# Average pooling by four: loads of 63 KB and one-piece stores in place of loads of 64 KB and two-piece stores

## The chip, the core and the metric

The kernel runs on one core of a Trainium2 chip. The metric is the device time of one execution in microseconds (us); shorter is better. The time before is the median of three runs, 1557.35 us (1557.14 to 1557.62).

A core has several engines that run side by side. Here VectorE (DVE) adds, ScalarE (ACT) multiplies by a quarter, and SyncE (SP) and ScalarE issue DMAs, which 16 DMA engines carry out between DRAM and the 128 partitions of the on-chip memory. DMAs issued by SP are on queue q1 of the profile, those issued by ACT on q10.

## What is computed

```python
def reference(x, kernel_size, stride):      # x: (64, 256, 8192) float32, both numbers are 4
    out_len = (length - kernel_size) // stride + 1
    for i in range(out_len):
        start = i * stride
        output[:, :, i] = np.mean(x[:, :, start : start + kernel_size], axis=2)
```

Window and stride are both 4 and 8192 is a multiple of 4, so every four neighbours of the flattened input give one output. The input is 536.87 MB, the output 134.22 MB.

## The kernel before

The flat input is cut into 64 blocks of 8 MB. In each block every one of the 128 partitions has a run of 16,384 contiguous elements (`RUN`, 64 KB), and gives 4,096 results (16 KB).

There are two input tiles `xt` of 64 KB per partition (pool `xin`) and two result tiles `r` of 2 x 16 KB (pool `res`); a tile is taken by turns, and its new writer waits until the readers of its old contents are done. The main loop takes two blocks to one result tile:

- `load` (L43) is issued by SP. Load i waits until the reduce of block i - 2 has freed its input tile.
- `sums` (L47) is one VectorE reduce that adds each group of four into a half of `r`. The first reduce into a result tile waits for the store that last read it, two groups ago.
- `scale` (L65) multiplies the whole of `r` by 1/4 on ScalarE, in place.
- The store (L77) is issued by ScalarE. Its DRAM side (`both`) has two 16 KB pieces for each partition, 2 MB apart, one in each block.

The last four blocks are handled apart. For the last group of the loop, scale and store come after the loads of the last two blocks have been issued, and the store goes through SP (L87). Block 62 is reduced, scaled and stored by itself (L90). Block 63 is loaded in two pieces of 10,240 and 6,144 elements (`LAST`); each is summed by `pair_sums`, two VectorE additions, scaled, and stored by SP (L95). `pair_sums` first adds neighbours in place, leaving the sums on every other element (L56), and then adds those sums in pairs, reading every fourth element (L60).

Each engine executes its instructions in program order. Nothing but the waits on tiles orders one engine against another.

Of the kernel before, what the change touches and what calls it, by code (L numbers as in the profile page):

```python
# [1 line left out]

# [4 lines left out]


RUN = 16384

LAST = (10240, 6144)


@with_exitstack
def kernel(
    ctx: ExitStack,
    tc: tile.TileContext,
    x: bass.AP,
    kernel_size: bass.AP,
    stride: bass.AP,  # L20
    out: bass.AP,
):
    nc = tc.nc
    K, S = int(kernel_size), int(stride)
    assert K == S == 4
    B, C, L = x.shape
    P = nc.NUM_PARTITIONS
    dt = x.dtype
    M = RUN // K
    blocks = B * C * L // (P * RUN)  # L30
    assert blocks * P * RUN == B * C * L and L % K == 0 and blocks % 2 == 0
    assert sum(LAST) == RUN

    xb = x.rearrange("b c l -> (b c l)").rearrange("(n p m) -> n p m", p=P, m=RUN)
    ob = out.rearrange("b c l -> (b c l)").rearrange("(n p m) -> n p m", p=P, m=M)

    pin = ctx.enter_context(tc.tile_pool(name="xin", bufs=2))
    pout = ctx.enter_context(tc.tile_pool(name="res", bufs=2))

    def load(i, a=0, b=RUN, xt=None):  # L40
        if xt is None:
            xt = pin.tile([P, RUN], dt, name="xt")
        nc.sync.dma_start(out=xt[:, a:b], in_=xb[i][:, a:b])  # L43
        return xt

    def sums(o, xt, a=0, b=RUN):
        nc.vector.tensor_reduce(  # L47
            out=o,
            in_=xt[:, a:b].rearrange("p (m k) -> p m k", k=K),
            axis=mybir.AxisListType.X,  # L50
            op=mybir.AluOpType.add,
        )

    def pair_sums(o, xt, a, b):
        v = xt[:, a:b].rearrange("p (m k) -> p m k", k=2)
        nc.vector.tensor_tensor(  # L56
            out=v[:, :, 0], in0=v[:, :, 0], in1=v[:, :, 1], op=mybir.AluOpType.add
        )
        w = xt[:, a:b].rearrange("p (m k) -> p m k", k=K)
        nc.vector.tensor_tensor(  # L60
            out=o, in0=w[:, :, 0], in1=w[:, :, 2], op=mybir.AluOpType.add
        )

    def scale(o):
        nc.scalar.mul(o, o, 1.0 / K)  # L65

    def both(i):
        return ob[i : i + 2].rearrange("n p m -> p n m")

    for i in range(0, blocks - 2, 2):  # L70
        r = pout.tile([P, 2, M], dt, name="r")
        for h in range(2):
            xt = load(i + h)
            sums(r[:, h, :], xt)
        if i < blocks - 4:
            scale(r[:])
            nc.scalar.dma_start(out=both(i), in_=r[:])  # L77

    n = blocks - 1
    t = pout.tile([P, 2, M], dt, name="r")  # L80
    xt = load(n - 1)
    xl = None
    edges = [sum(LAST[:j]) for j in range(len(LAST) + 1)]
    for a, b in zip(edges[:-1], edges[1:]):
        xl = load(n, a, b, xl)
    scale(r[:])
    nc.sync.dma_start(out=both(n - 3), in_=r[:])  # L87
    sums(t[:, 0, :], xt)
    scale(t[:, 0, :])
    nc.sync.dma_start(out=ob[n - 1], in_=t[:, 0, :])  # L90
    for a, b in zip(edges[:-1], edges[1:]):
        o = t[:, 1, a // K : b // K]
        pair_sums(o, xl, a, b)
        scale(o)
        nc.sync.dma_start(out=ob[n][:, a // K : b // K], in_=o)  # L95


# [1 line left out]
_INS = ['x', 'kernel_size', 'stride']  # L99
_OUTS = [((64, 256, 2048), 'float32')]  # L100

_NUMBERS = {'kernel_size': 4, 'stride': 4}


# [26 lines left out]
```

## Time and profile before

| | |
|---|---|
| median of the runs | 1557.35 us |
| the profiled execution | 1557.44 us |
| its span, first to last instruction | 1555.7 us |
| DVE busy | 1101.1 us, 71% |
| ACT busy | 226.6 us, 15% |
| one reduce of a block, L47 | 17.22 us, 63 of them |
| one scale of a group, L65 | 7.03 us, 31 of them |
| DMA from issue to landing, a 64 KB load | 31.0 us median |
| DMA from issue to landing, a store of a group (L77) | 49.5 us median |
| DRAM traffic over the span | 431 GB/s |

The span runs from the first to the last instruction of the program; the time of the execution is a little longer. "Busy" leaves out waiting and the issuing of DMAs. In a timeline line, the first number is the start, the second the duration, both in us; `SPq` and `ACTq` are the issuing of a DMA; the square bracket has the engine's idle time before the instruction and what ended it. In a line of stretches the columns are the stretch, its length, busy time and number of instructions of DVE, ACT and POOL, the clock of TensorE (not used here), the busy share of the DMA engines, and GB/s.

A packet, in this text, is one record of the DMA part of the trace: one DMA engine moving one partition's contiguous row. Each DMA also has 16 packets of 4 bytes that report its completion, one for each engine.

### The profile page before, as it was taken

The page shows a single profiled execution, that of the slowest core. Times are in us where ns is not written, and L with a number is a line of the kernel's source. Part 1 is how long each engine was busy: PE and PEld are TensorE (multiplying, and loading weights), DVE is VectorE, ACT ScalarE, POOL GpSimd, SP SyncE. Part 2 cuts the span into 40 slices and gives each one's busy share as a digit, 9 for nine tenths or more (in the row PEclk, how much of TensorE's full clock was granted, in tenths as well). Part 3 has the DMA queues.
Part 4 walks back from the last instruction along what each step waited for, and adds up shares of the span by engine and source line. Part 5 has one row for each costly group of instructions (what it writes and reads, how often), then busy time and mean ns, then how long its engine had stood idle before and what let it go on. Part 6 is the DMA issues. An engine that isn't in the chain of part 4 may idle for free.

```text
span 1555.7 us, 398 instructions
## 1 busy us (share of the span) xinstructions
DVE 1101.1 (71%) x67; ACT 226.6 (15%) x35; POOL 0.2 (0%) x4
## 2 busy tenths in 40 slices
DVE  4858667677676776767768677676786766867668
ACT  0110111101111001111011110111101111011111
POOL 0000000000000000000000000000000000000000
DMA  9999999999999999999999999999999999999999
GB/s 425 395 429 435 437 439 431 431 423 436 437 431 438 436 428 431 437 429 441 438 435 429 433 424 443 431 433 436 434 428 436 431 436 436 434 435 431 434 428 399
DMA packets 18227, 671.12 MB, mean 431 GB/s; under 512 B 1584, under 2 KB 1584, under 8 KB 1712
## 3 DMA queue, kind: packets, MB, share of 16 engines
q1 hardware_dynamic: 10064, 545.26, 81.1%
q10 hardware_dynamic: 8160, 125.83, 18.9%
q14 instruction: 3, 0.02, 0.0%
HBM read 536.87 MB, written 134.22 MB: 431 GB/s over the span
## 4 chain that ended last, share of the span: by engine, by line
DMA 64%; DVE 35%; ACT 1%; issue 0%; SPq 0%; DVEq 0%
DMA xt<-in_x_dram 60%; DVE r L47 34%; DMA out_dram<-r 3%; DVE xt L56 1%; ACT r L65 1%; DVE r L60 0%; SPq L43 0%; DVEq L47 0%
## 5 line engine op out<-in xcount | busy, mean ns | idle before, releaser
L47 DVE TENSOR_REDUCE r<-xt 128x4096 f32<-128x16384 f32 x63 | 1084.8, 17220 | 448.5 <-DMA out_dram<-r 241.4
L65 ACT ACTIVATE r<-r 128x8192 f32<-128x8192 f32 (+3 forms) x34 | 225.3, 6628 | 1323.8 <-DVE r L47 1313.5
L56 DVE TENSOR_TENSOR xt<-xt 128x5120 f32<-128x5120 f32 (+1 forms) x2 | 8.8, 4420 | 0.0
L60 DVE TENSOR_TENSOR r<-xt 128x2560 f32<-128x2560 f32 (+1 forms) x2 | 7.6, 3776 | 0.1
L65 ACT ACT_TABLE_LOAD x1 | 1.3, 1283 | 0.7 <-PEq L112 0.7
L112 POOL MEMSET const-bfloat16-1.0<- 128x1 bf16 x1 | 0.1, 101 | 0.0
L112 POOL MEMSET const-uint8-127<- 128x1 uint8 x1 | 0.1, 101 | 0.0
L112 POOL MEMSET const-float32-0.0<- 128x1 f32 x1 | 0.1, 98 | 0.2 <-issue 0.2
L112 POOL MEMSET const-float32-1.0<- 128x1 f32 x1 | 0.1, 98 | 0.0
## 6 DMA issues: line engine op xcount, KB each, us to landing
out_dram<-r ACTq DMA_DIRECT2D x30, 4096.0 KB, 49.5
xt<-in_x_dram SPq DMA_DIRECT2D x1, 5120.0 KB, 19.6
out_dram<-r SPq DMA_DIRECT2D x1, 4096.0 KB, 29.6
xt<-in_x_dram SPq DMA_DIRECT2D x1, 3072.0 KB, 26.6
out_dram<-r SPq DMA_DIRECT2D x1, 2048.0 KB, 12.8
out_dram<-r SPq DMA_DIRECT2D x1, 1280.0 KB, 7.0
xt<-in_x_dram SPq DMA_DIRECT2D x63, 31.0
out_dram<-r SPq DMA_DIRECT2D x1, 768.0 KB, 3.5
```

The lines of the kernel that those rows point to most:

```text
L47: nc.vector.tensor_reduce(out=o, in_=xt[:, a:b].rearrange("p (m k) -> p m k", k=K), axis=mybir.AxisListType.X, op=mybir.AluOpType.add,)
L56: nc.vector.tensor_tensor(out=v[:, :, 0], in0=v[:, :, 0], in1=v[:, :, 1], op=mybir.AluOpType.add)
L60: nc.vector.tensor_tensor(out=o, in0=w[:, :, 0], in1=w[:, :, 2], op=mybir.AluOpType.add)
L65: nc.scalar.mul(o, o, 1.0 / K)
L112: nc = _bacc.Bacc("TRN2", target_bir_lowering=False, num_devices=1)
```

## The change

- The run of a load becomes 16,128 elements (63 KB). Two loads, h = 0 and 1, now read the two halves of a run of 32,256 contiguous elements (126 KB) of each partition, so that the results of a group are 8,064 contiguous elements of DRAM for each partition. The store of a group has one piece of 31.5 KB for each partition.
- There are 32 such groups (64 loads). What is left of the input is one block of 16,384 contiguous elements for each partition (`END`), loaded in the same two pieces `LAST` as before.
- The first load of all is issued as two of 8,064 elements for each partition (`FIRST`), and each half is reduced when it has landed.
- `pair_sums` writes its first sums compactly to the front of the piece, and its second addition reads neighbours there, that is every other element.
- In the last group, each half is scaled by itself. Its second half is summed by `pair_sums` in place of the reduce. All its loads and those of the last block are issued ahead of its store, which goes through SP.

The tiles stay as they were in number: `xt` has 16,384 elements for each partition, `r` has 8,064.

```diff
-RUN = 16384
+RUN = 16128
+END = 16384
+FIRST = (8064, 8064)
 LAST = (10240, 6144)
...
-    xb = x.rearrange("b c l -> (b c l)").rearrange("(n p m) -> n p m", p=P, m=RUN)
-    ob = out.rearrange("b c l -> (b c l)").rearrange("(n p m) -> n p m", p=P, m=M)
+    xb = xf[:body].rearrange("(n p h m) -> n p h m", p=P, h=2, m=RUN)
+    ob = of[: body // K].rearrange("(n p m) -> n p m", p=P, m=2 * M)
+    xe = xf[body:].rearrange("(p m) -> p m", p=P)
+    oe = of[body // K :].rearrange("(p m) -> p m", p=P)
...
     def pair_sums(o, xt, a, b):
         v = xt[:, a:b].rearrange("p (m k) -> p m k", k=2)
+        h = xt[:, a : (a + b) // 2]
         nc.vector.tensor_tensor(
-            out=v[:, :, 0], in0=v[:, :, 0], in1=v[:, :, 1], op=mybir.AluOpType.add
+            out=h, in0=v[:, :, 0], in1=v[:, :, 1], op=mybir.AluOpType.add
         )
-        w = xt[:, a:b].rearrange("p (m k) -> p m k", k=K)
+        w = h.rearrange("p (m k) -> p m k", k=2)
         nc.vector.tensor_tensor(
-            out=o, in0=w[:, :, 0], in1=w[:, :, 2], op=mybir.AluOpType.add
+            out=o, in0=w[:, :, 0], in1=w[:, :, 1], op=mybir.AluOpType.add
         )
...
-    for i in range(0, blocks - 2, 2):
-        r = pout.tile([P, 2, M], dt, name="r")
+    for g in range(groups):
+        r = pout.tile([P, 2 * M], dt, name="r")
         for h in range(2):
-            xt = load(i + h)
-            sums(r[:, h, :], xt)
-        if i < blocks - 4:
+            xt = None
+            for a, b in edges(FIRST) if g + h == 0 else [(0, RUN)]:
+                xt = load(xb[g, :, h, :], a, b, xt)
+                o = r[:, h * M + a // K : h * M + b // K]
+                if g == groups - 1 and h == 1:
+                    pair_sums(o, xt, a, b)
+                else:
+                    sums(o, xt, a, b)
+                if g == groups - 1:
+                    scale(o)
+        if g < groups - 1:
             scale(r[:])
-            nc.scalar.dma_start(out=both(i), in_=r[:])
+            nc.scalar.dma_start(out=ob[g], in_=r[:])
...
-    scale(r[:])
-    nc.sync.dma_start(out=both(n - 3), in_=r[:])
-    sums(t[:, 0, :], xt)
-    scale(t[:, 0, :])
-    nc.sync.dma_start(out=ob[n - 1], in_=t[:, 0, :])
-    for a, b in zip(edges[:-1], edges[1:]):
-        o = t[:, 1, a // K : b // K]
+    for a, b in edges(LAST):
+        xl = load(xe, a, b, xl)
+    nc.sync.dma_start(out=ob[groups - 1], in_=r[:])
+    e = pout.tile([P, 2 * M], dt, name="r")
+    for a, b in edges(LAST):
+        o = e[:, a // K : b // K]
         pair_sums(o, xl, a, b)
         scale(o)
-        nc.sync.dma_start(out=ob[n][:, a // K : b // K], in_=o)
+        nc.sync.dma_start(out=oe[:, a // K : b // K], in_=o)
```

More of the change, by code (lines that the diff above doesn't have):

```diff
@@ L29, with load, sums @@
     M = RUN // K
-    blocks = B * C * L // (P * RUN)
-    assert blocks * P * RUN == B * C * L and L % K == 0 and blocks % 2 == 0
-    assert sum(LAST) == RUN
-    xb = x.rearrange("b c l -> (b c l)").rearrange("(n p m) -> n p m", p=P, m=RUN)
-    ob = out.rearrange("b c l -> (b c l)").rearrange("(n p m) -> n p m", p=P, m=M)
+    total = B * C * L
+    groups = total // (2 * P * RUN)
+    body = groups * 2 * P * RUN
+    assert L % K == 0 and total - body == P * END
+    assert sum(FIRST) == RUN and sum(LAST) == END
+    xf = x.rearrange("b c l -> (b c l)")
+    of = out.rearrange("b c l -> (b c l)")
+    xb = xf[:body].rearrange("(n p h m) -> n p h m", p=P, h=2, m=RUN)
+    ob = of[: body // K].rearrange("(n p m) -> n p m", p=P, m=2 * M)
+    xe = xf[body:].rearrange("(p m) -> p m", p=P)
+    oe = of[body // K :].rearrange("(p m) -> p m", p=P)
     pin = ctx.enter_context(tc.tile_pool(name="xin", bufs=2))
     pout = ctx.enter_context(tc.tile_pool(name="res", bufs=2))
-    def load(i, a=0, b=RUN, xt=None):
+    def load(src, a, b, xt=None):
         if xt is None:
-            xt = pin.tile([P, RUN], dt, name="xt")
-        nc.sync.dma_start(out=xt[:, a:b], in_=xb[i][:, a:b])
+            xt = pin.tile([P, END], dt, name="xt")
+        nc.sync.dma_start(out=xt[:, a:b], in_=src[:, a:b])
         return xt
-    def sums(o, xt, a=0, b=RUN):
+    def sums(o, xt, a, b):
         nc.vector.tensor_reduce(
@@ L65, in scale, with edges @@
         nc.scalar.mul(o, o, 1.0 / K)
-    def both(i):
-        return ob[i : i + 2].rearrange("n p m -> p n m")
-    for i in range(0, blocks - 2, 2):
-        r = pout.tile([P, 2, M], dt, name="r")
-        for h in range(2):
-            xt = load(i + h)
-            sums(r[:, h, :], xt)
-        if i < blocks - 4:
+    def edges(cuts):
+        at = [sum(cuts[:j]) for j in range(len(cuts) + 1)]
+        return list(zip(at[:-1], at[1:]))
+    for g in range(groups):
+        r = pout.tile([P, 2 * M], dt, name="r")
+        for h in range(2):
+            xt = None
[9 more added lines that the diff above has]
+        if g < groups - 1:
             scale(r[:])
[L77 to L81, printed above, removed]
+            nc.scalar.dma_start(out=ob[g], in_=r[:])
     xl = None
-    edges = [sum(LAST[:j]) for j in range(len(LAST) + 1)]
-    for a, b in zip(edges[:-1], edges[1:]):
-        xl = load(n, a, b, xl)
-    scale(r[:])
-    nc.sync.dma_start(out=both(n - 3), in_=r[:])
-    sums(t[:, 0, :], xt)
-    scale(t[:, 0, :])
-    nc.sync.dma_start(out=ob[n - 1], in_=t[:, 0, :])
-    for a, b in zip(edges[:-1], edges[1:]):
-        o = t[:, 1, a // K : b // K]
+    for a, b in edges(LAST):
[4 more added lines that the diff above has]
+        o = e[:, a // K : b // K]
         pair_sums(o, xl, a, b)
         scale(o)
-        nc.sync.dma_start(out=ob[n][:, a // K : b // K], in_=o)
+        nc.sync.dma_start(out=oe[:, a // K : b // K], in_=o)
 _INS = ['x', 'kernel_size', 'stride']
```

## The prediction, made before the result was known

> **What bounds the kernel now.** I read the page first, its engines and its DMA lines:
>
> ```profile
> span 1555.7 us, 398 instructions
> ...
> DVE 1101.1 (71%) x67; ACT 226.6 (15%) x35; POOL 0.2 (0%) x4
> ...
> DMA packets 18227, 671.12 MB, mean 431 GB/s; under 512 B 1584, under 2 KB 1584, under 8 KB 1712
> ...
> q1 hardware_dynamic: 10064, 545.26, 81.1%
> q10 hardware_dynamic: 8160, 125.83, 18.9%
> ```
>
> No compute engine is busy for the whole span; the two DMA queues are, 81.1 + 18.9%. The view by stretches says where that holds (the last two columns are the busy share of the DMA engines and GB/s):
>
> ```profile
> 0.00:40.00 40.00, 17.22 (x1) 1.28 (x1) 0.20 (x4) 1.00 0.98 419
> 40.00:80.00 40.00, 33.43 (x2) 7.03 (x1) 0.00 (x0) 1.00 0.97 398
> 400.00:1400.00 1000.00, 711.60 (x42) 143.46 (x21) 0.00 (x0) 1.00 1.00 434
> 1510.00:1550.00 40.00, 33.44 (x5) 11.66 (x4) 0.00 (x0) 1.00 0.99 425
> 1550.00:1556.00 6.00, 0.00 (x0) 1.18 (x1) 0.00 (x0) 1.00 0.54 223
> ```
>
> The middle runs at 434 GB/s with a share of 1.00; time is lost at both ends alone. The trace also records each packet (one partition's row of a DMA). Median ns by bytes: 611 for 16,384, 1514 for 40,960, 2418 for 65,536. The slope, (2418 - 611)/49,152, is 27.2 bytes per ns for each of 16 engines; all 671.12 MB at that rate take 671.12e6/16/27.2 = **1542.1 us**. No edit here moves fewer bytes, so the change can only touch the remaining 13.6 us of the span.
>
> The chain of waits calls DVE 35% and DMA 64% of the span, and the view of waits has 241.4 us of DVE waiting for stores. Neither limits the middle, as its timeline shows:
>
> ```profile
> 1467.08 0.38 ACTq L77 DMA_DIRECT2D out_dram<-r  x1
> 1468.33 17.22 DVE L47 TENSOR_REDUCE r<-xt 128x4096 f32<-128x16384 f32 x1 [8.34 <-DMA out_dram<-r]
> 1485.57 0.33 SPq L43 DMA_DIRECT2D xt<-in_x_dram  x1
> 1491.12 17.22 DVE L47 TENSOR_REDUCE r<-xt 128x4096 f32<-128x16384 f32 x1 [5.57 <-DMA xt<-in_x_dram]
> ```
>
> A load is issued at 1485.57 when a reduce frees its buffer, while the load ahead of it lands only at 1491.1: the queue holds 5.5 us of work. From 46 to 1500 us the packet records leave the 16 engines idle 0.03 us on average.
>
> **The change, term by term.**
>
> *Packets.* Before: 65 loads of 128 rows (8,320) and stores of 30 x 256 + 256 + 128 + 2 x 128 = 8,320, because each partition's two 16 KB results lie in two places in DRAM. After: 67 loads (8,576), and 32 stores of 128 rows of 31.5 KB plus 256 at the end (4,352). Data packets fall from 16,640 to 12,928, by 232 per engine; the 4-byte completion packets (16 per DMA, 99 DMAs to 101) rise by 2 per engine; net 230. A packet's price beyond its bytes: the packet rows give 611 - 16,384/27.2 = 8.6 ns, but packets overlap a little. From the store issued at 354.55 to that at 789.76 are nine periods, 48.357 us each; a period is 1,310,720 bytes per engine, 48.188 us; the other 0.169 us over 16 + 16 + 3 packets is 4.8 ns each. I take 4.8, the measured throughput: 230 x 4.8 ns = **-1.1 us**. Ends: 0 (if a 31.5 KB row is cut; against that, 40,960-byte rows are single packets) and 230 x 8.6 = -2.0.
>
> The Trainium skill ("DMA: Bandwidth & Descriptors", Why small descriptors are slow) gives a fixed overhead of about three cycles per packet; at the 850 MHz it names that is 3.5 ns, an estimate of -0.8 us by the page. The 4.8 ns measured here is a little more, and the sum goes by the measurement.
>
> *The dry spot at 40 us.* Its rows:
>
> ```profile
> 22.56 17.22 DVE L47 TENSOR_REDUCE r<-xt 128x4096 f32<-128x16384 f32 x1 [22.56 <-DMA xt<-in_x_dram]
> 39.80 0.33 SPq L43 DMA_DIRECT2D xt<-in_x_dram  x1
> 41.88 17.22 DVE L47 TENSOR_REDUCE r<-xt 128x4096 f32<-128x16384 f32 x1 [2.10 <-DMA xt<-in_x_dram]
> ```
>
> Load 2 is issued at 39.80, load 1's last packet ends at 41.52, and load 2's first packets start from 41.11 to about 43: the 16 engines lose 1.04 us on average, and load 2's packets run 0.61 us longer per engine than their median, the first on each engine about 3.0 us instead of 2.4. Load 3 (issued 59.13, an early engine reaching it at 61.14) has 1.11 us of such excess. Sum 2.76.
> With a first load in halves, half of reduce 0 (16.95/2 = 8.5 us) is done while the second half comes in, and load 2 is issued near 31, ten us ahead. But load 3 waits for reduce 1, which waits for all of load 1: reduce 1 ends 0.35 (landing) + 16.95 + 0.05 = 17.35 us after load 1's last packet, and load 2 takes 8 x 2.380 = 19.04 (2.380 = 64,512/27.2 + 8.6 ns). That leaves 1.7 us; before, load 2 had 41.52 - 39.80 = 1.7. The gap moves by one load. What goes is the second, since load 4 is issued about 8 us ahead, the first store then sharing the engines: **-1.1 us**. Ends: 0 and -2.76.
>
> *The tail.* Now:
>
> ```profile
> 1516.15 17.22 DVE L47 TENSOR_REDUCE r<-xt 128x4096 f32<-128x16384 f32 x1 [7.81 <-DMA out_dram<-r]
> ...
> 1546.79 2.87 DVE L60 TENSOR_TENSOR r<-xt 128x1536 f32<-128x1536 f32 x1
> 1549.69 1.48 ACT L65 ACTIVATE r<-r 128x1536 f32<-128x1536 f32 x1 [3.83 <-DVE r L60]
> ```
>
> DVE starts the last full block at 1516.15, when an old store frees its result tile, and all later sums queue behind it; the last store is issued at 1551.20. The engines are idle 0.63 us between 1545 and 1552.3.
> After: L56 rows (5.483 us for 5,120, 3.357 for 3,072) make 1.038 ns per element plus 0.17. Reading compact pairs with the same step, the second sums cost 2.83 and 1.76 us instead of 4.685 and 2.867; at worst L60's own rate stays. The last body half costs 8.54 + 4.35 = 12.9 us (15.8 at L60's rate) instead of 16.95. From the landing of the last load to the last store's issue: at most 1.0 (piece one's 8.3 against 7.3 of transfer) + 3.36 + 1.76 + 1.48 = 7.6 us. Behind that load lie the store of the last group, 8 x 1.195 = 9.6 us, and the piece of 10,240-byte rows, 8 x 0.385 = 3.1. The 12.7 cover it, and cover about 9 us at L60's rate too: **-0.6 us**, ends 0 and -1.0 (the remaining skew of the engines with it).
>
> *What costs nothing or little.* The split load adds one issue (0.4 us of SP, with nothing due) and 9 packets per engine, counted above. Scales, now two on the last group (3.6 us each), end before the last load lands. A store needs 8 rounds of one load packet and one store packet, 8 x (2.380 + 1.195) = 28.6 us, where 16 rounds took 48.4; so the 241.4 us of DVE's waits on stores vanish, and nothing is won: loads are late next, and the engines are full.
>
> Sum: -1.1 - 1.1 - 0.6 = -2.8 against the profiled 1557.44 (span 1555.7 and 1.7 around it), 0.09 above the median of 1557.35: **1554.6 us**.
>
> **The rivals.**
>
> *More (0.22):* packets at 8.6 ns and a start without a dry spot: -2.0 - 2.76 - 0.6 = -5.4, 1552.0. For: the price of a cold packet may sit in load 2 alone. Against: the 1.7 us above.
>
> *Gain eaten (0.10):* each added transfer costs time of its own. Nearest row: 39.80 to 41.11, 1.31 us from issue to first packet; two added loads 2.6, so 1557.2. Against: load 1's first packet starts at 21.74 while load 0's last ends at 22.18; behind a filled queue there is no gap.
> The Trainium skill ("SBUF — State Buffer", The DMA setup-cost knee) has about 2 us per transfer that does not shrink with bytes; two more would be +4 us, an estimate of 1558.6 by the page. It speaks against this change; the trace shows that latency only where a queue is empty.
>
> *Slower (0.08):* the lead gets too thin in the middle. Now each load meets store packets all along, 24.2 us. After, 19 us of each period of 2 x 8 x 2.380 + 8 x 1.195 = 47.6 have no store. A store's first packet follows the odd reduce's end by 6.92 + 3.6 + 0.1 = 10.6 us. If the preceding load ends x after that reduce, the odd load takes 28.6 - 0.5 (10.6 - x), and the loop closes with x + that time = 47.6 - 17.4: x = 4.6, against 5.5 now. Descriptors reached the engines 1.3 to 3.5 us after the issue at 39.80, so 4.6 holds; it decides if the slowest engine's lead falls under about 2. Price: load 2's 0.61 us in each of 31 periods, +18.9 - 2.8: 1573.5.
>
> **How the numbers follow.** Forecast 0.60. A measurement of this kernel can tell about 0.2% (3.1 us) from no change, so the bound is 1554.24 and the forecast lies 0.4 short of it; by its terms' ends I give 0.16 of its 0.60 to the far side. Faster 0.16 + 0.22 = 0.38, same 0.44 + 0.10 = 0.54, slower 0.08. The range takes the forecast, the first rival and the second, and leaves the third: 1552.0 to 1557.5.
>
> **What would show it.** Packets 12,928 + 1,616 + a few of instructions, about 14,550; 434 to 435 GB/s in the middle, periods of about 47.6 us; no DVE wait on stores; load 2 issued near 31 us and a dry spot near 60; the last store issued before the one ahead of it ends. It is wrong if the middle falls under 433 GB/s (thin lead), if packets of 64,512 bytes take more than 2.39 us, or if the first 80 us run without a gap.

## The result, and the profile after

The changed kernel takes **1559.48 us** (median of 20 runs, 1557.20 to 1567.22) against 1557.28 us before (20 runs, 1556.62 to 1557.95). The ratio is 1.002, 95% interval 1.0013 to 1.0027: slower, by about the 0.2% that the prediction named as its bound, and by 2.2 us going by the medians. It lies outside the range of 1552.0 to 1557.5. As telling as the median is the scatter, 10 us where before had 1.3. The traced execution is the slowest of the 20, 1567.22 us. Its page, the same lines as shown of before:

```profile
span 1565.4 us, 409 instructions
...
DVE 1094.5 (70%) x70; ACT 226.8 (14%) x36; POOL 0.2 (0%) x4
...
DMA packets 14547, 671.12 MB, mean 429 GB/s; under 512 B 1616, under 2 KB 1616, under 8 KB 1744
...
q1 hardware_dynamic: 10080, 543.10, 80.9%
q10 hardware_dynamic: 4464, 127.99, 18.9%
...
out_dram<-r ACTq DMA_DIRECT2D x31, 4032.0 KB, 32.4
```

The packets fell from 18,227 to 14,547, as forecast, and a group's store now lands in 32.4 us instead of 49.5. The view of waits has for the reduces, before and then after:

```profile
DVE r L47 <- DMA out_dram<-r: 241.4, 29, 12.8
DVE r L47 <- DMA xt<-in_x_dram: 207.2, 34, 22.6
```

```profile
DVE r L55 <- DMA xt<-in_x_dram: 450.9, 64, 13.1
```

The 241.4 us on stores are gone, and the reduces wait for loads alone.

The time went somewhere else. By stretches (last column GB/s):

```profile
40.00:80.00 40.00, 33.91 (x2) 6.92 (x1) 0.00 (x0) 1.00 1.01 417
200.00:400.00 200.00, 140.69 (x9) 27.69 (x4) 0.00 (x0) 1.00 1.00 424
400.00:600.00 200.00, 138.54 (x10) 34.62 (x5) 0.00 (x0) 1.00 1.00 427
600.00:800.00 200.00, 145.35 (x9) 27.69 (x4) 0.00 (x0) 1.00 1.00 434
1200.00:1400.00 200.00, 145.28 (x9) 27.69 (x4) 0.00 (x0) 1.00 1.00 434
```

Between 200 and 600 us the kernel moves 424 to 427 GB/s, then 434 like before. The busy share is 1.00 in both parts, so that column hides the loss: packets take longer, and a slow packet counts as busy. The packet records of the traces give an account of each span, in us per DMA engine (the median is that of all packets of the same size in the same trace):

| | before | changed |
|---|---|---|
| all packets at the median of their size | 1551.9 | 1549.6 |
| overlap of successive packets | -4.3 | -3.1 |
| time above the median, first 100 us | 2.4 | 2.6 |
| time above the median, later | 0.2 | **11.2** |
| engines idle | 2.4 | 2.0 |
| ahead of the first and behind the last packet | 3.0 | 3.2 |
| span | 1555.7 | 1565.4 |

So 11 us are slow packets in the middle, and everything else changed by less than 2.5 us. They come in every period (from one store's issue to the next) up to the store issued at 504.58 and hardly after: periods there last 48.4 to 49.1 us, later 47.6 (one of them 48.3). A period of each kind, in the timeline:

```profile
303.29 0.33 SPq L51 DMA_DIRECT2D xt<-in_x_dram  x1
303.29 6.92 ACT L74 ACTIVATE r<-r 128x8064 f32<-128x8064 f32 x1 [42.18 <-DVE r L55]
307.83 16.95 DVE L55 TENSOR_REDUCE r<-xt 128x4032 f32<-128x16128 f32 x1 [4.57 <-DMA xt<-in_x_dram]
310.24 0.34 ACTq L95 DMA_DIRECT2D out_dram<-r  x1
...
640.41 0.33 SPq L51 DMA_DIRECT2D xt<-in_x_dram  x1
640.42 6.92 ACT L74 ACTIVATE r<-r 128x8064 f32<-128x8064 f32 x1 [40.65 <-DVE r L55]
644.90 16.95 DVE L55 TENSOR_REDUCE r<-xt 128x4032 f32<-128x16128 f32 x1 [4.52 <-DMA xt<-in_x_dram]
647.37 0.34 ACTq L95 DMA_DIRECT2D out_dram<-r  x1
```

For the program they are the same: a load issued as the second reduce of a group ends, 4.5 us before the load ahead of it has landed, and a store issued 7 us after the load. The packet records differ. In the first, the load's first packets start 1.39 to 4.05 us after its issue, a spread of 2.7 us over the engines; five of them take 2.65 to 2.97 us instead of 2.38, and around the store's first packets (314.15 to 317.19) a load packet on every engine is slow, up to 3.55 us. In the second, the first packets start 2.64 to 4.01 us after the issue, and no packet is slow. I call the time from a load's issue to the first packet of any engine its **lead**, 1.39 and 2.64 us here.

### The profile page after: what moved, and what is told of

It reads as the page before. It is cut to its first block, busy times and chain, and to the rows that moved or that the text cites. A ratio compares the mean times of both kernels' runs of the same rounds, so it can differ in the third digit from the quotient of the medians.

```text
span 1565.4 us, 409 instructions
## 1 busy us (share of the span) xinstructions
DVE 1094.5 (70%) x70; ACT 226.8 (14%) x36; POOL 0.2 (0%) x4
## 2 busy tenths in 40 slices
DMA packets 14547, 671.12 MB, mean 429 GB/s; under 512 B 1616, under 2 KB 1616, under 8 KB 1744
## 3 DMA queue, kind: packets, MB, share of 16 engines
q10 hardware_dynamic: 4464, 127.99, 18.9%
## 4 chain that ended last, share of the span: by engine, by line
DMA 64%; DVE 35%; issue 0%; ACT 0%; DVEq 0%; SPq 0%
DMA xt<-in_x_dram 64%; DVE r L55 34%; DVE xt L65 1%; DVE r L69 0%; ACT r L74 0%; DVEq L55 0%; SPq L51 0%; DVEq L69 0%
## 5 line engine op out<-in xcount | busy, mean ns | idle before, releaser
L55 DVE TENSOR_REDUCE r<-xt 128x4032 f32<-128x16128 f32 (+1 forms) x64 | 1068.2, 16691 | 450.9 <-DMA xt<-in_x_dram 450.9
L74 ACT ACTIVATE r<-r 128x8064 f32<-128x8064 f32 (+3 forms) x35 | 225.6, 6444 | 1330.1 <-DVE r L55 1302.5
L65 DVE TENSOR_TENSOR xt<-xt 128x8064 f32<-128x8064 f32 (+2 forms) x3 | 17.4, 5801 | 10.7 <-DMA xt<-in_x_dram 10.7
L69 DVE TENSOR_TENSOR r<-xt 128x4032 f32<-128x4032 f32 (+2 forms) x3 | 8.9, 2981 | 0.2
## 6 DMA issues: line engine op xcount, KB each, us to landing
out_dram<-r ACTq DMA_DIRECT2D x31, 4032.0 KB, 32.4
```

The lines of the kernel that those rows point to most:

```text
L55: nc.vector.tensor_reduce(out=o, in_=xt[:, a:b].rearrange("p (m k) -> p m k", k=K), axis=mybir.AxisListType.X, op=mybir.AluOpType.add,)
L65: nc.vector.tensor_tensor(out=h, in0=v[:, :, 0], in1=v[:, :, 1], op=mybir.AluOpType.add)
L69: nc.vector.tensor_tensor(out=o, in0=w[:, :, 0], in1=w[:, :, 1], op=mybir.AluOpType.add)
```

## The experiments

Three theories were set against each other, the third after the first runs. **Lead:** the load that follows a group's second reduce is queued too late for the engines that are ahead of the others. **Rows:** rows of 63 KB, 126 KB apart, are read worse. **Store timing:** a store that sets in too soon after a load's start, while loads run alone, makes packets slow. "Above the median" is time per engine in packets above the median of their size, after the first 100 us; before has 0.2.

| kernel | median (lowest to highest) | ratio to before, 95% | above the median |
|---|---|---|---|
| one_piece_64 | 1557.40 (1556.02 to 1561.68) | 0.9998 to 1.0015 | 1.7 |
| two_piece_63 | 1557.32 (1556.97 to 1558.06) | 0.9992 to 1.0009 | 0.1 |
| pair_all | 1570.66 (1564.89 to 1572.67) | 1.0066 to 1.0093 | 16.2 |
| scale_twice | 1556.89 (1556.03 to 1557.44) | 0.9989 to 1.0006 | 0.4 |
| short_reduce | 1571.08 (1569.54 to 1572.98) | 1.0078 to 1.0109 | 12.6 |
| pair_scale_twice | 1554.85 (1554.63 to 1555.09) | 0.9977 to 0.9994 | 0.4 |
| scale_halves | 1619.41 (1618.12 to 1622.88) | 1.0389 to 1.0417 | 51.0 |
| late_store_pair_head | **1554.38** (1554.31 to 1557.46) | 0.9975 to 0.9993 | 0.4 |
| store_on_sp | 1558.47 (1557.99 to 1558.92) | 0.9999 to 1.0017 | 1.3 |
| scale_plus | 1556.69 (1556.46 to 1558.39) | 0.9990 to 1.0008 | 0.5 |
| late_whole_first | 1557.92 (1556.81 to 1559.04) | 0.9996 to 1.0014 | 1.8 |
| late_strided_sums | 1556.65 (1556.33 to 1557.56) | 0.9988 to 1.0006 | 0.5 |
| pair_scale_halves | 1567.66 (1560.91 to 1575.04) | 1.0047 to 1.0095 | 19.2 |
| thin_lead_late_store | 1560.65 (1559.33 to 1568.41) | 1.0019 to 1.0042 | 5.0 |
| after_again | 1562.87 (1558.64 to 1567.35) | 1.0022 to 1.0044 | 11.1 |

**Is it the rows?** One kernel has one-piece stores and loads of 64 KB, one the reverse; the views of the output follow those of the input.

```diff
 one_piece_64 (from the kernel before)
+    xg = flat[:body].rearrange("(n p h m) -> n p h m", p=P, h=2, m=RUN)    # RUN is 16384
+    og = out.rearrange("b c l -> (b c l)")[: body // K].rearrange("(n p m) -> n p m", p=P, m=2 * M)
```

> The kernel before, with one edit: the two loads of a group read the halves of one 128 KB run of each partition, so its store is one piece of 32 KB; loads stay 64 KB, the head and the last blocks stay as they were. Theory 1 (thin lead): a store that takes 28 us instead of 48 lets the loads between stores run alone, the load that follows a group's second reduce is queued only some 4.5 us before the load ahead of it lands, its packets come late; then this kernel shows the same slow stretch as the changed one: packets above their median worth 3 us or more per engine, runs that scatter over several us, a median of 1557.5 to 1561. Theory 2 (rows of 63 KB at 126 KB distance are read worse): nothing of that here, packets above their median under 3 us as before, all runs within 1 us, median near 1556 (only fewer packets).

```diff
 two_piece_63 (from the changed kernel)
-    xb = xf[:body].rearrange("(n p h m) -> n p h m", p=P, h=2, m=RUN)
+    xb = xf[:body].rearrange("(n h p m) -> n h p m", p=P, h=2, m=RUN)
```

> The changed kernel with its groups cut into two separate blocks, so that every load is 63 KB at 63 KB distance and each store has two pieces of 15.75 KB again; the rest as changed. Theory 1 (thin lead): stores last the whole period again, the lead is 5.5 us or more, no slow stretch after the first 80 us, runs within 1 us, median 1556 to 1557.5. Theory 2 (rows of 63 KB): packets above their median worth 5 us or more per engine, scatter of several us, median about 1559.5.

Loads of 63 KB with two-piece stores: 1557.32 us, runs within 1.1 us, no slow packets. Loads of 64 KB with one-piece stores: 5.7 us of scatter and slow periods up to the third, though the traced run lost only 1.7 us where 3 or more were expected. The size of the loads is not the cause. The two kernels with slow packets share the short store, which leaves the loads alone for 19 us of each period, and rows 126 or 128 KB apart. The distance drops out with scale_twice and pair_scale_twice below, which read the same rows as the changed kernel and lose 0.4 us; the short store remains.

**More lead.** VectorE gives each input tile back 4 us sooner.

```diff
 pair_all
-                if g == groups - 1 and h == 1:
+                if b - a == RUN:
```

> The changed kernel with pair_sums for every whole block instead of the reduce: 12.9 us of VectorE per block instead of 16.95, so each input tile is free 4 us sooner. Theory 1 (thin lead): the thin lead of 4.4 us becomes about 8, the slow stretch goes, periods of 47.6 us from the second group on, runs within 1 us, median 1554 to 1555.5. Theory 2 (rows and addresses): DMA addresses and their order are the same, so the slow stretch stays, median about 1559.5 with scatter of several us.

```diff
 short_reduce (leaves out a quarter of the sums; that part of the result tiles is set to zero once)
-                    sums(o, xt, a, b)
+                    c = a + 12288 if b - a == RUN else b
+                    sums(r[:, h * M + a // K : h * M + c // K], xt, a, c)
```

> The changed kernel with the reduce of each whole block over 12,288 of its 16,128 elements; a quarter of the sums is left out (set to zero once). VectorE then takes about 12.9 us per block, as long as pair_sums, but by a reduce. Lead theory: with 4 us more lead no slow stretch, median 1555 to 1556; the run with pair_sums everywhere speaks against it already. Store-timing theory (the packets around a store's first ones are slow when the store meets a load that began less than some 10 us before): store and load meet as with pair_sums everywhere, median 1564 to 1573. Traffic theory (the in-place additions of VectorE disturb the DMAs): no slow stretch, median 1555 to 1557.

Both are slower than the changed kernel, by 11 us. VectorE frees the tiles sooner in every block, but the lead stays large in the first third of the run only; what that leaves of the lead theory is told with its table below. Short VectorE work is enough for it, in whatever instruction, so memory traffic of the additions is not needed. In pair_all the loss is now spread over the whole span:

```profile
200.00:400.00 200.00, 106.48 (x17) 31.41 (x5) 0.00 (x0) 1.00 1.01 431
600.00:800.00 200.00, 106.45 (x17) 27.69 (x4) 0.00 (x0) 1.00 1.00 430
```

**Moving the store.** Nothing but ScalarE's work ahead of the store is changed: two passes (7 us later), a pass and a half (3.5 us later), or each half scaled as soon as it is summed (3.4 us earlier).

```diff
 scale_twice
-            scale(r[:])
+            for _ in range(2):
+                nc.scalar.mul(r[:], r[:], 0.5)
 scale_plus
             scale(r[:])
+            nc.scalar.mul(r[:, :M], r[:, :M], 1.0)
 scale_halves
-                if g == groups - 1:
-                    scale(o)
-        if g < groups - 1:
-            scale(r[:])
+            o = r[:, h * M : (h + 1) * M]
+            scale(o)
```

> The changed kernel with each group scaled in two passes by 1/2 instead of one by 1/4: 7 us more of ScalarE per group, and its store issued 7 us later. Theory 1 (thin lead): the store then overlaps the thin load's predecessor as much as the other one, by the same loop as in the prediction the two leads are about 6.9 and 5.9 us instead of 4.6 and 8.2; the slow stretch goes although there is more work, runs within 1.5 us, median 1554 to 1556. Theory 2 (rows and addresses): no change, median about 1559.5 with scatter. If ScalarE's work itself mattered: slower than the changed kernel.

> The changed kernel with one more ScalarE pass (times 1.0) over half of each group, so that the store is issued 3.5 us later than in the changed kernel. A dose between 0 (median 1559.5, scatter of 10 us) and 7 us (1556.9, scatter of 1.4). Store-timing theory: no slow stretch or a short one, median 1555.5 to 1557.5, scatter under 3 us. If only the whole 7 us help: as the changed kernel, 1558 to 1561.

> The changed kernel with each half of a group scaled as soon as it is reduced, so the store is issued 3.4 us earlier. Lead theory: by the loop of the prediction the thin lead falls from 4.6 to 3.5 us, and the slow stretch lasts through the whole run: 31 periods of 1 us or more, median 1565 to 1590. Store-timing theory: the store meets its load 6 us after its first packets instead of 9.5, slow in most periods too, median 1562 to 1575. If neither: as the changed kernel, 1559.5 with scatter.

This is the dose: 3.4 us earlier 1619.4, as changed 1559.5, 3.5 us later 1556.7, 7 us later 1556.9. ScalarE does twice the work in scale_twice and the kernel is 2.6 us faster and steady. For scale_halves both theories had expected 1590 at most: its traced run has 51 us of slow packets and 14 us of idle engines (2 in the changed kernel). By stretches, scale_halves first, then scale_plus:

```profile
200.00:400.00 200.00, 137.05 (x9) 28.50 (x8) 0.00 (x0) 1.00 1.00 418
600.00:800.00 200.00, 138.07 (x9) 28.50 (x8) 0.00 (x0) 1.00 1.00 420
```

```profile
200.00:400.00 200.00, 139.54 (x10) 50.25 (x10) 0.00 (x0) 1.00 1.00 434
600.00:800.00 200.00, 140.23 (x9) 41.94 (x8) 0.00 (x0) 1.00 1.00 433
```

But the store's time sets the lead too, by the loop worked out in the prediction: the lead is about 1 us in most periods of scale_halves, 3.0 in scale_plus (mean of the periods), 1.3 to 2.65 in the first trace of the changed kernel. The next runs set the two against each other.

**Lead against store timing.**

```diff
 pair_scale_twice: pair_all and scale_twice together
 pair_scale_halves: pair_all and scale_halves together
 thin_lead_late_store: scale_twice, and a side reduce ahead of each whole one
+                        sums(side[:], xt, a, a + 2304)
                     sums(o, xt, a, b)
```

> Pair_sums for every whole block, and each group scaled in two passes, so that the store is issued 7 us later. Store-timing theory: the store meets its load some 12 us after that load's first packets instead of 5, so most slow packets go: median 1555 to 1559. Traffic theory: the additions are the same, median 1565 or more. Lead theory: leads stay above 6 us, 1555.

> Thick lead, early store: pair_sums for every whole block (each load issued 4 us sooner) and each half of a group scaled by itself (each store issued 3.6 us after a load instead of 7). Lead theory: between pair_sums everywhere (1570.7) and the changed kernel, far below the 1619.4 of halves scaled alone, since the lead is 4 us larger. Store-timing theory: worse than pair_sums everywhere, since the store comes sooner after the load: 1580 to 1620. If both matter: 1571 to 1600.

> Thin lead, late store: the scale in two passes (store issued 7 us later) with a side reduce of 2,304 elements before each block's reduce, 2.55 us more of VectorE per whole block, its sums used nowhere. Each load is issued 2.5 us later: with the store late its first packets came 3.9 us after its issue, now about 1.4, as in the slow stretch of the changed kernel. Store-timing theory: no slow packets around the store's first ones, only the first packets of loads late on some engines; median 1557 to 1560 (0 to 0.1 us per period). Lead theory: slow stretches as in the changed kernel or worse, 1562 to 1590.

With the store late, pair_sums everywhere is clean (1554.85, runs within 0.5 us; lead 6.4 or more). With the store early, more lead takes 52 us off scale_halves (1567.7), against the store-timing theory taken alone, yet does not make it clean. With the store late and less lead, the first periods are slow while the lead is 1.4 to 2.5 us, and clean once it is 2.7: against the store-timing theory too. Neither theory stands alone. The packet records of the kernels with the whole reduce and one-piece stores through ScalarE (ten traces of nine kernels, groups 1 to 28, 280 periods, each from one load that follows a group's second reduce to the next such load), sorted by the lead of that load:

| lead, us | periods | mean time above the median per period, us |
|---|---|---|
| under 1.5 | 35 | 1.61 |
| 1.5 to 2.0 | 13 | 1.06 |
| 2.0 to 2.5 | 13 | 0.34 |
| 2.5 to 3.0 | 93 | 0.03 |
| over 3.0 | 126 | 0.01 |

In these kernels the loss goes with the lead, with a step between 2 and 2.5 us; 26 of the 35 periods in the first row are those of scale_halves. The spread of the engines by itself does not make packets slow: 97 periods with a spread of 2 us or more and a lead over 2.5 lose 0.02 us on average. Nor does an early store by itself explain the changed kernel: its store is always issued 6.96 us after the load, and in the clean periods of the first trace its first packet follows the load's sooner (7.7 to 8.0 us in most) than in the slow ones (9.0 to 10.2).

In the four with shorter VectorE work a large lead is not enough: periods with a lead over 3.0 still lose up to 0.76 us in pair_all, short_reduce and pair_scale_halves, where the store's first packet comes 2.4 to 7.2 us after the load's; in pair_scale_twice, where it comes 8.7 us or more after, 0.07 at most. But those are only 27 of the 84 periods of the first three kernels. In each of them the engines drift apart and the lead shrinks: in pair_all the spread grows from 0.4 to 4.8 us and the lead falls from 7.5 to 2.1. The other 57 periods have leads of 1.6 to 3.0 and lose 0.63 us on average, against 0.29 in the 27. So most of what these kernels lose comes with a thin lead after all, and the early store is needed for the part before it. That the slow packets at the early store drive the engines apart and so thin the lead fits this order of events, but no run shows it. What in the DMA engines makes the packets slow under either condition stays open.

**One queue.** The store goes through SP, behind the next group's loads, with no added work.

```diff
 store_on_sp
+        if late is not None:
+            nc.sync.dma_start(out=ob[g - 1], in_=late[:])
+        late = r
         if g < groups - 1:
             scale(r[:])
-            nc.scalar.dma_start(out=ob[g], in_=r[:])
```

> The changed kernel with each group's store issued by SP, behind the loads of the next group, so that loads and stores are one queue and no store packet comes between the packets of a load; no added work. The store is still issued 7 us after a load. If the slow packets come from a second queue setting in while loads run alone: none here in the middle, runs within 1 us, median 1553.5 to 1555.5. If a store issued within 7 us of a load is enough, in whatever queue: slow stretches and scatter as in the changed kernel, 1557 or more.

The middle is clean (1.3 us above the median after the first 100 us), but the median is 1558.47, since the end of the kernel is no longer covered by transfers. The engines are idle 2.8 us after 1490 us, against 0.8 in the changed kernel:

```profile
1510.00:1550.00 40.00, 27.03 (x7) 10.95 (x4) 0.00 (x0) 1.00 0.98 425
1550.00:1558.00 8.00, 0.00 (x0) 0.00 (x0) 0.00 (x0) 1.00 0.35 143
```

In this order a load that follows a group's second reduce is issued, at 624.2 us for one, 11.7 us before the load ahead of it has landed (635.9), instead of 4.4. So the run has more lead as well and doesn't separate the theories; it shows that a clean middle needs no added work.

**A version that beats both.** Late stores in the groups 1 to 29 only, so that the last one isn't late, and pair_sums for block 1, so that load 3 is issued sooner.

```diff
 late_store_pair_head
-                if g == groups - 1 and h == 1:
+                if b - a == RUN and (g == 0 or g == groups - 1 and h == 1):
-            scale(r[:])
+            if 0 < g < groups - 2:
+                for _ in range(2):
+                    nc.scalar.mul(r[:], r[:], 0.5)
+            else:
+                scale(r[:])
```

> The changed kernel with the second scale pass in the groups 1 to 29 only, and pair_sums for block 1 (and the last, as changed). With the scale in two passes everywhere the middle was clean, but 1.4 us of idle engines were added at the end, because the last of these stores came late, and the first 100 us still lost 2.2 us. Expected, if both go: 1556.9 - 1.4 - 1.5 = 1554.0 median, 1553.5 to 1555.5, all runs within 1.5 us. If store timing does not keep the middle clean: 1556 or more with scatter.

1554.38 us, ratio to before 0.9984 (0.9975 to 0.9993), though one of the 11 runs took 1557.46, outside the expected 1.5 us. Its stretches:

```profile
40.00:80.00 40.00, 29.87 (x3) 6.92 (x1) 0.00 (x0) 1.00 1.04 439
200.00:400.00 200.00, 141.13 (x9) 65.05 (x10) 0.00 (x0) 1.00 1.00 434
600.00:800.00 200.00, 138.00 (x10) 55.38 (x8) 0.00 (x0) 1.00 1.00 435
```

The 40 us after the start now move as much as the middle. With the middle clean, the two small parts of the change can be priced by taking each out.

```diff
 late_whole_first
-FIRST = (8064, 8064)
+FIRST = (16128,)
 late_strided_sums
-            out=h, in0=v[:, :, 0], in1=v[:, :, 1], op=mybir.AluOpType.add
+            out=v[:, :, 0], in0=v[:, :, 0], in1=v[:, :, 1], op=mybir.AluOpType.add
```

> The version with late stores and pair_sums for block 1 (1554.4), with its first load whole again. By the prediction the split moves the dry spot by one load and saves the second one: without it, a median of 1555 to 1556.5. If the split gains nothing: 1554.4 or a little less.

> The version with late stores and pair_sums for block 1 (1554.4), with the sums of pair_sums left on every other element again (the second addition reads every fourth). By the prediction the last sums are covered by stores still in the queue: at L60's old rate the tail keeps its cover, 1554.4 within 0.4. If the compact sums shorten the end: 1555 to 1556.

Without the split of the first load this version is 3.5 us slower, without the compact sums 2.3. Only part of the 3.5 lies at the start: by the two traces, 4.1 us apart, 1.4 us are idle engines and slow packets of the first 100 us, 1.3 are slow packets later (late_whole_first loses 1.8 there, not 0.4), and 1.4 are engines idle after 1490 us. So its middle isn't wholly clean, and why its end costs more isn't shown. What the compact sums do, the end of late_strided_sums shows, then that of late_store_pair_head:

```profile
1545.44 5.66 SPq L109 DMA_DIRECT2D out_dram<-r  x2
1546.35 2.87 DVE L68 TENSOR_TENSOR r<-xt 128x1536 f32<-128x1536 f32 x1
1549.25 1.48 ACT L73 ACTIVATE r<-r 128x1536 f32<-128x1536 f32 x1 [3.84 <-DVE r L68]
```

```profile
1540.82 4.54 SPq L110 DMA_DIRECT2D out_dram<-r  x2
1541.73 1.76 DVE L69 TENSOR_TENSOR r<-xt 128x1536 f32<-128x1536 f32 x1
1543.52 1.48 ACT L74 ACTIVATE r<-r 128x1536 f32<-128x1536 f32 x1 [2.73 <-DVE r L69]
```

With the strided sums the last store is issued at 1550.76, after the packets of the one ahead have ended (1550.19); with the compact ones at 1545.03, while they run until 1549.43. The engines' idle time after 1490 us is 2.9 and 0.9 us.

**A second trace of the changed kernel.**

> The changed kernel as it is, for a second trace: the first trace was the slowest of its runs. Expected: 1557 to 1563, and the packets above their median after the first 100 us account for the run's distance from 1555.5 within 1 us; the slow stretch ends at another time than in the first trace, and does not come back once the periods are 47.6 us.

Its runs have a median of 1562.87. The traced one is as slow as the first (span 1565.6), and again the loss is in packets above their median, 11.1 us, with nearly all of it in the periods up to 505 us; later ones lose 0.12 us at most. The end of the slow stretch fell at the same time in both traces, against the expectation. An execution near the median has not been traced. The same kernel had a median of 1559.48 at first and of 1562.87 here, while the kernel before stayed between 1557.03 and 1557.28 beside all these runs; differences of a few us from the changed kernel therefore rest on the scatter and the packet records as well, not on one median alone.

## Why the prediction was wrong

- **Packets, -1.1 us: right.** In the account, the medians fall by 2.3 us and the overlap by 1.2, which leaves -1.1.
- **The start, -1.1: too large in this kernel.** Load 2 was issued at 31.25 and the gap moved to load 3 (issued 58.70, first packets from 59.85), as worked out. But load 3 alone then lost 1.83 us above its median; idle and slow packets of the first 100 us went from 3.8 to 3.5 us only. In late_store_pair_head, where block 1 is also freed sooner, leaving out the split costs 3.5 us, of which 1.4 are at the start.
- **The end, -0.6: not seen.** Idle time after 1490 us went from 1.0 to 0.8 us, and the time behind the last packet rose by 0.2. The cover by queued stores held with the compact sums: the last store was issued at 1557.70 in the first trace, while the one ahead ran until 1562.11. That it would hold at L60's old rate was wrong by 2.3 us (late_strided_sums). The step counted only the last piece's sums; those of the first piece (4.69 us at L60's rate, 2.83 compact) and of the half block, queued ahead on VectorE, grow as well.
- **The middle, 0: this is the step that failed.** The sum put nothing for the shorter store, because loads are late next "and the engines are full". They were full, with a share of 1.00, but of slow packets: 11.2 us per engine in the traced run, and a middle of 424 to 427 GB/s where the prediction itself had named less than 433 as a sign of being wrong. It had the thin lead as its third rival, and the loop that gave a lead of 4.6 us came out: a load is issued 4.4 us before the one ahead lands. It failed in how it used the number. It took one lead for all 16 engines and let it decide "if the slowest engine's lead falls under about 2". In the runs the loss goes with the engine that is first to finish: the engines are up to 3 us apart, most periods are slow when the first of them reaches the new load within 2 us of its issue, and none of the changed kernel's is when that takes 2.5 us or more. The 0.08 for this case came from that reading.
- **Its price** was 18.9 us, 0.61 in each of 31 periods. Measured were 0.95 to 1.6 us in most of the periods of a slow stretch, but the stretch ended by itself: some 11 us in the slowest runs, and by the medians of 1559.5 and 1562.9 against 1556.7 (scale_plus) some 3 to 6 us in a usual one. Most of it lies at the store's first packets, not at the load's, and that the prediction did not have at all.
- **The sum of the other terms** was 1554.6; late_store_pair_head, with the middle put right and block 1 freed sooner, takes 1554.38. Much of that agreement is luck: the terms of the start and the end were off in both directions, and block 1's sooner release is no part of the sum.
- **The pages.** By the Trainium skill ("SBUF — State Buffer", The DMA setup-cost knee) each added transfer would cost some 2 us. No such price shows here: in late_whole_first one transfer fewer costs 3.5 us more, and in the middle of late_store_pair_head, from 100 to 1490 us, the engines are idle 0.05 us in all. The Trainium skill ("DMA: Bandwidth & Descriptors", Issuing engines are not separate DMA queues) says that issuing from several engines only saves time on their sequencers. The transfers do share the engines here, but issuing the store 7 us later, which changes the leads too, was worth 63 us (scale_halves against scale_plus).

## What to carry to other kernels

When a kernel is bound by transfers, a shorter store may not be free: here it changed which packets meet, and left loads alone that had met store packets all along. Work out the lead of every load in the new rhythm, and compare it not as a mean but for the DMA engine that runs ahead. Here, runs that scattered over some seven times the spread of the kernel before went with a lead near its edge, and work added on an idle engine to move a store was a remedy.

## What was not expected of the hardware

- A slow packet shows as a busy DMA engine: the share stays at 1.00 while the rate falls from 434 to 418 GB/s (scale_halves). Only the durations of packets show it.
- The loss comes late. In the slow periods of the changed kernel's first trace, from group 1 on, 0.0 to 0.2 us are lost on a load's first packets, and 0.8 to 1.4 us some 7 to 15 us after its issue, when the store's first packets come; in the period shown above on all 16 engines. Why there is not shown.
- The slow rhythm can end by itself. At the store issued at 504.58 the spread of the engines at a load's start shrinks from 2.4 to 2.0 us, then to 1.4, the lead grows to 2.6 us, and the periods stay at 47.6 us but for one. With the lead at about 1 us (scale_halves) it never ended.
